# One encoder layer on one core: both heads' products with v as one item of the order, first loads and splits ordered anew, six pairs of the first feed-forward layer begun with plain products

## The chip, the cores and the metric

The kernel runs on one NeuronCore of one Trainium2 chip. The metric is the device time of one execution in microseconds (us). Times come from several runs; one further execution is recorded by the hardware profiler, instruction by instruction, and the rows below come from that one.

## What is computed

One layer of a bidirectional encoder over 1024 positions of width 1024, in float32:

```
z = rms_norm(x) @ W_in + b_in          # split into q | k | v | u | y_branch | g_att | g_rec
y_att = neighbourhood_attention(q, k, v, rpb) @ w_att_o      # 8 heads of 64
y_rec = ((rg_lru forward + rg_lru backward)(conv(u)) * gelu(y_branch)) @ w_rec_o
x = x + (sigmoid(g_att) * y_att + sigmoid(g_rec) * y_rec) @ w_out
x = x + square(relu(rms_norm(x) @ w_ff1)) @ w_ff2
out = rms_norm(x)
```

The attention works on 64 tiles of 128 queries by 384 keys: four pairs of heads (m), two halves of the grid (hf), four column blocks (n), and the two heads of the pair (hd). The probabilities of a tile are multiplied with the v of 384 gathered keys of 64 columns each.

## The kernel before, in words

**Products.** TensorE multiplies pairs of float32r numbers: each operand is split into a high part (a rounded copy, made by ScalarE, sometimes by VectorE) and a low part (the rest, made by VectorE), and a product is three matmuls, high by high, high by low, low by high. The product with W_in (without v's columns) and both feed-forward products are done in seven block products instead of eight. `pairs` does this for a pair of weight blocks: the plain products A11·B11 and A12·B21 need only the first half of the positions, while the five others, S2·T2, S1·T1, S3·T3, S4·B22 and A22·T4, use sums and differences of blocks, which need all positions. The first `pre` pairs do their two plain products ahead of everything else, two pairs at a time; every later pair does its seven in a row. A pair keeps its first bank of PSUM (key 0) from A11·B11 to A22·T4. Before, the `pairs` call of the first feed-forward layer has `pre` 4, that of W_in has 2. A plain product is 12 matmuls of 128x512.

**The order.** Nothing is issued in program order. Every operation is recorded in a `Plan` with a position: a list of products (`main`, one unit of position for each) and side work at fractional positions (`SD(pos, fn, boost)`, a boost moves it ahead). `Plan.solve` is a list scheduler: with its own costs for each operation it lets each engine take, at each moment, the operation with the lowest position among those whose inputs are ready, and hands out the buffers ("t" has 45 tiles of 512 KB in SBUF, "w" 9, PSUM has "pm" 2, "pr" 2, "pa" 4 banks). A bank or a "w" tile is handed out in the order of positions. `Plan.issue` then writes each engine's instructions in the order found. On the chip each engine, and SP's queue, which issues all DMAs, runs that fixed order and waits where an input is late. A transfer's end is estimated from `dma[0]`, when the queue is free, a rate and a latency.

**The start.** x comes in eight tiles (`load_x`), v's weights in four (`wvj`). A tile is squared and summed (`norm1_a`, ScalarE), scaled (`norm1_b`, VectorE, by a chain of small operations, `rstd_chain`), transposed on TensorE against an identity, and split (`put_0` for tiles 0 to 3, `put_F` and `put_D` for 4 to 7). v is the first product. The weights' high parts are made by VectorE for the parts in `WD`, by ScalarE otherwise.

**The attention.** A tile passes `a_qk` (two matmuls, then VectorE and ScalarE make the probabilities), `a_norm`, `a_tr` (three transposes, then ScalarE copies them out of PSUM) and `a_av`. `a_av` runs once for a pair of tiles, head 0 and head 1: three steps b, in each a matmul for head 0 into the lower 64 partitions of a bank and one for head 1 into the upper 64. In the trace each of these plain float32 matmuls leaves two records, so that a pair has 12. Each matmul waits for its own head's transposed tile alone. The attention's positions lie among the 64 steps of the product with w_rec_o (`tprod`, six matmuls a step), which fills TensorE in between.

**The channel part.** x @ w_out is done in tiles of 128 positions; each finished tile is normalised (`ln2`), transposed in "pa" banks, and goes into the blocks B11, B21 (tiles 0 to 3) or the sums T1 to T4 and B22 (tiles 4 to 7) of the first feed-forward product.

Of the kernel before, what the change touches and what calls it, by code (L numbers as in the profile page):

```python
# [10 lines left out]
P = 128  # L11
# [95 lines left out]
class Plan:  # L107


    def __init__(self, slots):  # L110
        self.ops, self.slots, self.pos, self.boost = [], slots, 0.0, 0.0
        self.last_alloc, self.last_tab = {}, None
        self.talloc, self.reserve, self.mark = [], 4, None
        self.late, self.rlate, self.gated = 1e9, 2, False

    def engine(self, name):
        return _Eng(self, name)
# [1 line left out]
    def add(self, eng, meth, args, kw):  # L119
# [21 lines left out]
        for v in wr:  # L141
            t = v.base
            if not t.ops:
                op.alloc.append(t)
                t.first = op.idx
                if t.tag == "t":
                    self.talloc.append(op.idx)
                elif t.tag not in "scd":
                    if t.tag in self.last_alloc:
                        op.preds.setdefault(self.last_alloc[t.tag], 0)  # L150
                    self.last_alloc[t.tag] = op.idx
            for o, b in t.writes:
                if _hit(b, v.box):
                    op.preds[o.idx] = 1
            for o, b in t.reads:
                if o is not op and _hit(b, v.box):
                    op.preds[o.idx] = 1
            t.writes = [(o, b) for o, b in t.writes if not all(x[0] >= y[0] and x[1] <= y[1]
                                                              for x, y in zip(b, v.box))]
            t.writes.append((op, v.box))  # L160
            t.ops.add(op.idx)
        op.preds.pop(op.idx, None)
        if eng == "pe":
            self.mark = op.idx
# [43 lines left out]
    def solve(self):  # L208
# [13 lines left out]
        av = {e: [] for e in engs}  # L222
        parked = {}
        cur = [None]
        dma = [0.0]

        tnext = [0]
        wait = []
# [42 lines left out]
        while done < len(ops):  # L271
# [23 lines left out]
            tfree[e] = s + c  # L295
            op.end = s + c
            if op.bytes:
                dma[0] = max(dma[0], s + 900) + op.bytes / 330.0
                op.end = dma[0] + 1200
            done += 1  # L300
            for t in op.tiles:
                k = id(t)
# [45 lines left out]
def emit(tc, x, prm, wst, wv, wg, watt, wrec, wout, wff1, wff2, tb, bv, lnf, out):  # L348
# [6 lines left out]
    with ExitStack() as ctx:  # L355
# [18 lines left out]
        def PM():  # L374
            return VT(nm("pm"), (P, 512), F32, "pm")
# [63 lines left out]
        dve.memset(epst, EPS)  # L439
        act.activation(s1("tab"), epst, AF.Sqrt)  # L440
        SD(-98, lambda: sp.dma_start(pr, prm))

        def softplus():
            lam = pr[:, PC["lam"]:PC["lam"] + 16]
# [143 lines left out]
        def prod(o, a, ob, b, key, bank, first, ev, boost=5.0):  # L588

            for kk in range(2):  # L590
                def run(kk=kk):
                    if kk == 0 and first:
                        o.ps[key] = PM() if bank else PA()
                    hi, lo = o.lhs[a]()
                    ps = o.ps[key]
                    for k in (2 * kk, 2 * kk + 1):
                        bh, bl = ob[b]["h"][kk][:, k % 2, :], ob[b]["l"][kk][:, k % 2, :]
                        pe.matmul(ps, hi[:, k, :], bh, start=(first and k == 0), stop=False, skip_group_check=True)
                        pe.matmul(ps, hi[:, k, :], bl, start=False, stop=False, skip_group_check=True)
                        pe.matmul(ps, lo[:, k, :], bh, start=False, stop=(k == 3), skip_group_check=True)  # L600
                last = M(run)
            SD(last + 0.1, lambda: ev(o, o.ps[key]), boost)
# [28 lines left out]
            o.store(o.r1, 1)  # L631
            o.store(o.r0, 0)

        def pairs(srcs, stores, ob, pre):

            ps_ = []
            for st in stores:
                o = Obj()
                o.r0, o.store, o.ps = None, st, {}
                ps_.append(o)  # L640
            st = here()
            for i in range(pre):
                pjob(ps_[i], srcs[i], st + 4 * i, st + 4 * pre + 10 * i)
            for i0 in range(0, pre, 2):
                g = ps_[i0:min(i0 + 2, pre)]
                for o in g:
                    prod(o, "A11", ob, "B11", 0, i0 == 0, True, ev1, 30.0)
                for o in g:
                    prod(o, "A12", ob, "B21", 1, False, True, ev2, 30.0)
            for i, o in enumerate(ps_):  # L650
                if i >= pre:
                    pjob(o, srcs[i], here(), here() + 2)
                    prod(o, "A11", ob, "B11", 0, True, True, ev1, 10.0)
                    prod(o, "A12", ob, "B21", 1, False, True, ev2)
                prod(o, "S2", ob, "T2", 0, False, False, ev6)
                prod(o, "S1", ob, "T1", 2, False, True, ev5)
                prod(o, "S3", ob, "T3", 0, False, False, ev7)
                prod(o, "S4", ob, "B22", 2, False, False, ev3)
                prod(o, "A22", ob, "T4", 0, False, False, ev4)
                o.end = here()  # L660
            return [o.end for o in ps_]

# [1 line left out]
            return len(main)  # L664

        hT = Half("hT")
        PRE1, ND, NB = 2, 1, 0.0
        WD, P0B, P0N = (0, 1, 2), 4.0, 2

        xt = [None] * 8  # L670

# [14 lines left out]
        def norm1_b(t):  # L686
            o = nrm[t]
            r = rstd_chain(o.ss, o.s)
            dve.tensor_scalar(o.h, xt[t], r, None, ALU.mult)

        wvj = []
        for i in range(4):
            o = Obj()
# [13 lines left out]
                dve.tensor_sub(o.lo, o.st, o.hi)  # L707

            SD(-90 + i, dma)
            SD((-9, -6, -2.4, -2.3)[i], sp_)  # L710
        SD(-99, lambda: load_x(0))
        SD(-86.5, lambda: sp.dma_start(bvb, bv.unsqueeze(0).broadcast_to((P, 512))))
        for t in range(1, 8):
# [119 lines left out]
                ("g", 4), ("y", 3), ("g", 5), ("u", 3), ("g", 6), ("g", 7), ("qk", 0), ("qk", 1), ("qk", 2), ("qk", 3))  # L833
        FIRST = {"u": 8, "y": 16, "g": 24}
        STORE = {"u": st_u, "y": st_y, "g": st_g, "qk": st_qk}
        RSTEP, RRATE, AOFF, ASTEP = 33.0, 1.0, 1.0, 0.75
        B0 = here()
        ends = pairs([(wst[i], wst[4 + i]) if k == "qk" else (wst[FIRST[k] + 2 * i], wst[FIRST[k] + 2 * i + 1])
                      for k, i in PORD], [STORE[k](i) for k, i in PORD], ob1, PRE1)
# [225 lines left out]
        def a_tr(o):  # L1065
            pt = PA()
            for b in range(3):
                pe.transpose(pt[:, b * P:(b + 1) * P], o.p[:, b * P:(b + 1) * P], ident)
            o.pt = o.t
            act.activation(o.pt, pt[:, :384], AF.Copy)  # L1070

        avb = {}

        def a_av(o0, o1):
            if o0.n == 0:
                avb[0] = PA()
            ps = avb[0]
            for b in range(3):
                g = b + o0.hf
                for o in (o0, o1):  # L1080
                    pe.matmul(ps[o.hd * DH:(o.hd + 1) * DH, o.n * P:(o.n + 1) * P],
                              V[o.m][g // 2][:, g % 2, o.n, o.hd * DH:(o.hd + 1) * DH],
                              o.pt[:, b * P:(b + 1) * P], start=(b == 0), stop=(b == 2))
            if o0.n == 3:
                m, hf = o0.m, o0.hf
                if hf == 0:
# [9 lines left out]
        for s in range(nt):  # L1096
            o = tiles[s]
            if o.n % 2 == 0 and o.hd == 0:
                if s < 4:
                    SD(o.pos - 6, lambda o=o: b_load(o.m, o.hf, o.n // 2))  # L1100
                else:
                    SD(tiles[s - 4].pos + 0.1, lambda o=o: b_load(o.m, o.hf, o.n // 2))
            SD(o.pos, lambda o=o: a_qk(o))
            nxt = [tiles[s + d].pos if s + d < nt else tiles[-1].pos + (s + d - nt + 1) * ASTEP for d in range(4)]
            SD(nxt[1] + 0.1, lambda o=o: a_norm(o))
# [16 lines left out]
            split(rT[k].hi, rT[k].lo, rec[k])  # L1122

        for k in range(8):
            SD(RO - 16 + 1.2 * k, lambda k=k: rec_load(k))
            SD(RO - 9 + 1.2 * k, lambda k=k: rec_split(k))

        def att_load(k):
            att[k] = T("att")
# [192 lines left out]
        def hid(i):  # L1322
            return 4 * (i // 2) + i % 2

        pairs([(wff1[hid(i)], wff1[hid(i) + 2]) for i in range(16)], [ff_store(i) for i in range(16)], ob2, 4)

# [286 lines left out]
```

## Time and profile before

| | |
|---|---|
| median of three runs | 1441.06 us (1440.65 to 1441.09) |
| the profiled execution's own time | 1440.83 us |
| its span, first to last instruction | 1439.0 us |
| TensorE busy | 1413.8 us (98% of the span), 6544 matmuls |
| VectorE, ScalarE busy | 1042.2 us (72%), 854.2 us (59%) |
| granted TensorE clock, mean | 0.998 |
| the 16 DMA engines | 229.04 MB, 159 GB/s in the mean |
| the chain that ended last, by engine | TensorE 97%, DMA 1%, VectorE 1%, ScalarE 1% |

TensorE's busy time is the union of matmuls whose ends are modelled, each shown with its whole passage through the array; the distance from one start to the next tells what a matmul costs the engine. Nearly all instructions are recorded by one helper and so carry one line number (L336); they are told apart by the names of the tiles that they write and read.

### The profile page before, as it was taken

The numbers are of one execution on the slowest core, as the hardware profiler recorded it, in microseconds if no ns is written. First come the engines' busy times: TensorE is split into PE (matmuls) and PEld (weight loads), VectorE is DVE, ScalarE is ACT, GpSimd is POOL, SyncE is SP. The second block draws the span as 40 slices with busy tenths as digits, with TensorE's granted clock in tenths as the row PEclk, the third lists the DMA queues.
The fourth block names the chain that finished last, engine by engine and source line by source line (L and its number), as shares of the span: only waits on it lengthen the run. The fifth ranks groups of instructions, "written<-read, shape, count | busy, mean of one in ns | idle before, by whom it ended". The sixth has DMA issues, their size and how long they took to land.

```text
span 1439.0 us, 17698 instructions
## 1 busy us (share of the span) xinstructions
PE 1413.8 (98%) x6544; PEld 1159.2 (81%) x6544; DVE 1042.2 (72%) x1590; ACT 854.2 (59%) x1321; POOL 0.7 (0%) x6
## 2 busy tenths in 40 slices
PE   6999999999999999999999999999999999999997
PEld 5878888888888877777888788888888888888886
DVE  6897688896986777664855776666655877858996
ACT  7758786878668766654526555455555634322544
POOL 0000000000000000000000000000000000000000
PEclk9999999999999999999999999999999999999999
DMA  6523234234224866544903325444447883245402
GB/s 214 146 74 132 103 103 146 83 123 146 102 90 157 310 220 233 176 166 181 399 31 117 117 92 194 161 161 161 161 153 256 303 331 118 90 151 200 140 22 103
DMA packets 86936, 229.04 MB, mean 159 GB/s; under 512 B 8513, under 2 KB 16833, under 8 KB 86849
## 3 DMA queue, kind: packets, MB, share of 16 engines
q1 hardware_dynamic: 86848, 227.91, 45.5%
q8 instruction: 51, 0.84, 0.2%
q14 instruction: 37, 0.30, 0.1%
HBM read 158.67 MB, written 69.21 MB: 158 GB/s over the span
## 4 chain that ended last, share of the span: by engine, by line
PE 97%; DMA 1%; DVE 1%; ACT 1%; issue 0%; SPq 0%
PE pa L336 56%; PE pm L336 33%; PE pr L336 8%; DMA x<-in_x_dram 1%; DMA ws<-in_wv_dram 0%; ACT h L336 0%; DVE T4l L336 0%; DVE T1l L336 0%; ACT hTh L336 0%; DVE h L336 0%; ACT r L336 0%; DVE sl L336 0%; ACT ns L336 0%; DVE nu L336 0%; ACT F L336 0%
## 5 line engine op out<-in xcount | busy, mean ns | idle before, releaser
L336 PE MATMUL pa<-wh,rh 128*128 128x512 f32 x448 | 173.9, 389 | 0.0
L336 PE MATMUL pa<-wh,rl 128*128 128x512 f32 x448 | 173.9, 389 | 0.0
L336 PE MATMUL pa<-wl,rh 128*128 128x512 f32 x448 | 173.8, 389 | 0.0
L336 ACT ACTIVATE r<-r 128x1024 f32<-128x1024 f32 x64 | 67.7, 1060 | 68.2 <-DVE r L336 66.9
L336 ACT ACTIVATE r<-pm 128x512 f32<-128x512 f32 x102 | 60.4, 592 | 73.7 <-PE pm L336 72.8
L336 DVE TENSOR_TENSOR sl<-ws,sh 128x1024 fp32r<-128x1024 f32 x72 | 87.4, 1221 | 22.9 <-ACT sh L336 22.9
L336 ACT ACTIVATE rh<-rs 128x1024 fp32r<-128x1024 f32 x56 | 58.5, 1048 | 67.1 <-PE pa L336 53.5
L336 PEld LDWEIGHTS pa<-wh,rh 128*128 128x128 f32 x448 | 84.1, 188 | 17.5
L336 PEld LDWEIGHTS pa<-wh,rl 128*128 128x128 f32 x448 | 84.1, 188 | 17.5
L336 PEld LDWEIGHTS pa<-wl,rh 128*128 128x128 f32 x448 | 84.1, 188 | 17.3
L336 ACT ACTIVATE wh<-w 128x1024 fp32r<-128x1024 f32 x56 | 58.8, 1051 | 60.2 <-PE pa L336 43.9
L336 ACT ACTIVATE sh<-ws 128x1024 fp32r<-128x1024 f32 x72 | 75.6, 1056 | 31.0 <-DVE ws L336 25.1
L336 DVE TENSOR_TENSOR wl<-ws,wh 128x1024 fp32r<-128x1024 f32 x64 | 77.5, 1218 | 17.1 <-ACT wh L336 16.5
L336 PE MATMUL pm<-T4h,wx 128*128 128x512 f32 x272 | 89.5, 389 | 0.0
L336 DVE TENSOR_TENSOR r<-pa,r 128x512 f32<-128x512 f32 x74 | 50.9, 688 | 50.2 <-PE pa L336 48.3
L336 DVE TENSOR_TENSOR acc<-pa,acc 128x512 f32<-128x512 f32 x72 | 49.4, 688 | 50.4 <-PE pa L336 50.3
L336 DVE TENSOR_TENSOR wl<-w,wh 128x1024 fp32r<-128x1024 f32 x56 | 68.2, 1219 | 10.1 <-ACT wh L336 6.7
L336 ACT ACTIVATE wh<-ws 128x1024 fp32r<-128x1024 f32 x61 | 64.0, 1055 | 13.4 <-DMA ws<-in_wff_dram 6.8
L336 DVE TENSOR_TENSOR rl<-rs,rh 128x1024 fp32r<-128x1024 f32 x56 | 68.2, 1219 | 5.2 <-ACT rh L336 3.0
L336 DVE CUSTOM_DVE_ANT_0 ab<-pa,B 128x384 f32<-128x384 f32 x64 | 35.4, 556 | 39.6 <-PE pa L336 38.8
L336 PEld LDWEIGHTS pm<-T4h,wx 128*128 128x128 f32 x272 | 51.1, 188 | 10.6
L336 ACT ACTIVATE ab<-pa 128x384 f32<-128x384 f32 x64 | 31.0, 484 | 45.6 <-PE pa L336 45.4
(242 smaller groups left out, 3776.1 us busy)
## 6 DMA issues: line engine op xcount, KB each, us to landing
rs<-rd SPq DMA_DIRECT2D x56, 512.0 KB, 6.6
ws<-in_wst_dram SPq DMA_DIRECT2D x41, 512.0 KB, 4.1
ws<-in_wff_dram SPq DMA_DIRECT2D x36, 512.0 KB, 4.5
w<-in_wff_dram SPq DMA_DIRECT2D x32, 512.0 KB, 7.5
B<-in_tb_dram SPq DMA_DIRECT2D x32, 384.0 KB, 4.6
x<-in_x_dram SPq DMA_DIRECT2D x16, 512.0 KB, 9.0
gd<-r SPq DMA_DIRECT2D x16, 512.0 KB, 2.9
g<-gd SPq DMA_DIRECT2D x16, 512.0 KB, 8.2
```

Of the source, the lines that this page charges most:

```text
L336: getattr(eng[op.eng], op.meth)(*[r(a) for a in op.args], **{k: r(a) for k, a in op.kw.items()})
```

## The change

`a_av` makes all six matmuls of a pair of tiles wait for both heads' transposed tiles (`plan.also`). 24 transposes of the identity are added at the very start (`warm`). The estimate of transfers in the scheduler is changed (700 ns, 290 bytes/ns and 1500 ns in place of 0, 330 and 1200), the positions of the first two v splits and the boosts of the first tiles are changed, ScalarE makes the high parts of all of v's weights, and VectorE the second copy of two tiles in place of one. The loads of the attention's bias tiles are six tiles ahead in place of four, the loads and splits of the recurrent branch's result lie earlier, and the attention's positions are moved ahead by 7 units. In the first feed-forward product six pairs begin with plain products in place of four; the first bank of pairs alternates between "pm" and "pr" (pairs 4 and 5 have theirs in "pa").

```diff
@@ -111,7 +111,7 @@
         self.talloc, self.reserve, self.mark = [], 4, None
-        self.late, self.rlate, self.gated = 1e9, 2, False
+        self.late, self.rlate, self.gated, self.also = 1e9, 2, False, ()
@@ -159,6 +159,8 @@
             t.ops.add(op.idx)
+        for o in self.also:
+            op.preds[o.idx] = 1
         op.preds.pop(op.idx, None)
@@ -222,7 +224,7 @@
         cur = [None]
-        dma = [0.0]
+        dma = [700.0]
@@ -295,8 +297,8 @@
             if op.bytes:
-                dma[0] = max(dma[0], s + 900) + op.bytes / 330.0
-                op.end = dma[0] + 1200
+                dma[0] = max(dma[0], s + 900) + op.bytes / 290.0
+                op.end = dma[0] + 1500
             done += 1
@@ -440,6 +442,14 @@
+        def warm():
+            ps = PA()
+            for _ in range(NWARM):
+                pe.transpose(ps[:, :P], ident, ident)
+
+        NWARM = 24
+        SD(-97, warm)
+
         def softplus():
@@ -590,7 +600,7 @@
                     if kk == 0 and first:
-                        o.ps[key] = PM() if bank else PA()
+                        o.ps[key] = VT(nm(bank), (P, 512), F32, bank)
                     hi, lo = o.lhs[a]()
@@ -631,12 +641,13 @@
-        def pairs(srcs, stores, ob, pre):
+        def pairs(srcs, stores, ob, pre, banks=("pm",)):
...
                 o.r0, o.store, o.ps = None, st, {}
+                o.bank = banks[len(ps_) % len(banks)] if len(ps_) < 2 * len(banks) or len(ps_) >= pre else "pa"
                 ps_.append(o)
@@ -644,19 +655,19 @@
                 for o in g:
-                    prod(o, "A11", ob, "B11", 0, i0 == 0, True, ev1, 30.0)
+                    prod(o, "A11", ob, "B11", 0, o.bank, True, ev1, 30.0)
                 for o in g:
-                    prod(o, "A12", ob, "B21", 1, False, True, ev2, 30.0)
+                    prod(o, "A12", ob, "B21", 1, "pa", True, ev2, 30.0)
             for i, o in enumerate(ps_):
...
                     pjob(o, srcs[i], here(), here() + 2)
-                    prod(o, "A11", ob, "B11", 0, True, True, ev1, 10.0)
-                    prod(o, "A12", ob, "B21", 1, False, True, ev2)
-                prod(o, "S2", ob, "T2", 0, False, False, ev6)
-                prod(o, "S1", ob, "T1", 2, False, True, ev5)
-                prod(o, "S3", ob, "T3", 0, False, False, ev7)
-                prod(o, "S4", ob, "B22", 2, False, False, ev3)
-                prod(o, "A22", ob, "T4", 0, False, False, ev4)
+                    prod(o, "A11", ob, "B11", 0, o.bank, True, ev1, 10.0)
+                    prod(o, "A12", ob, "B21", 1, "pa", True, ev2)
+                prod(o, "S2", ob, "T2", 0, None, False, ev6)
+                prod(o, "S1", ob, "T1", 2, "pa", True, ev5)
+                prod(o, "S3", ob, "T3", 0, None, False, ev7)
+                prod(o, "S4", ob, "B22", 2, None, False, ev3)
+                prod(o, "A22", ob, "T4", 0, None, False, ev4)
                 o.end = here()
@@ -664,8 +675,8 @@
         hT = Half("hT")
-        PRE1, ND, NB = 2, 1, 0.0
-        WD, P0B, P0N = (0, 1, 2), 4.0, 2
+        PRE1, PRE2, ND, NB = 2, 6, 2, 2.0
+        WD, P0B, P0N = (), 8.0, 4
@@ -688,6 +699,7 @@
+        W0P, W1P = -5.4, -5.2
         wvj = []
@@ -707,7 +719,7 @@
             SD(-90 + i, dma)
-            SD((-9, -6, -2.4, -2.3)[i], sp_)
+            SD((W0P, W1P, -2.4, -2.3)[i], sp_)
         SD(-99, lambda: load_x(0))
@@ -833,7 +845,7 @@
         STORE = {"u": st_u, "y": st_y, "g": st_g, "qk": st_qk}
-        RSTEP, RRATE, AOFF, ASTEP = 33.0, 1.0, 1.0, 0.75
+        RSTEP, RRATE, AOFF, ASTEP = 33.0, 1.0, -6.0, 0.75
         B0 = here()
@@ -1067,7 +1079,7 @@
             o.pt = o.t
-            act.activation(o.pt, pt[:, :384], AF.Copy)
+            o.done = act.activation(o.pt, pt[:, :384], AF.Copy)
@@ -1075,12 +1087,14 @@
             ps = avb[0]
+            plan.also = (o0.done, o1.done)
             for b in range(3):
...
                               o.pt[:, b * P:(b + 1) * P], start=(b == 0), stop=(b == 2))
+            plan.also = ()
             if o0.n == 3:
@@ -1096,10 +1110,10 @@
             if o.n % 2 == 0 and o.hd == 0:
-                if s < 4:
+                if s < 6:
                     SD(o.pos - 6, lambda o=o: b_load(o.m, o.hf, o.n // 2))
                 else:
-                    SD(tiles[s - 4].pos + 0.1, lambda o=o: b_load(o.m, o.hf, o.n // 2))
+                    SD(tiles[s - 6].pos + 0.1, lambda o=o: b_load(o.m, o.hf, o.n // 2))
             SD(o.pos, lambda o=o: a_qk(o))
@@ -1122,8 +1136,8 @@
         for k in range(8):
-            SD(RO - 16 + 1.2 * k, lambda k=k: rec_load(k))
-            SD(RO - 9 + 1.2 * k, lambda k=k: rec_split(k))
+            SD(RO - 24 + 2 * k, lambda k=k: rec_load(k))
+            SD(RO - 12 + 2 * k, lambda k=k: rec_split(k))
@@ -1322,7 +1336,7 @@
-        pairs([(wff1[hid(i)], wff1[hid(i) + 2]) for i in range(16)], [ff_store(i) for i in range(16)], ob2, 4)
+        pairs([(wff1[hid(i)], wff1[hid(i) + 2]) for i in range(16)], [ff_store(i) for i in range(16)], ob2, PRE2, ("pm", "pr"))
...

```

## Rows read from the trace of the kernel before

**Rows 1.** Windows of 36 us: length, busy us (instructions) of each engine, clock, DMA.
```profile
0.00:36.00 36.00, 24.42 (x109) 19.52 (x110) 23.71 (x75) 26.27 (x79) 0.70 (x6) 1.00 0.63 214
...
72.00:108.00 36.00, 34.32 (x149) 27.48 (x148) 32.93 (x78) 19.87 (x26) 0.00 (x0) 1.00 0.24 73
108.00:144.00 36.00, 36.00 (x160) 29.80 (x160) 27.19 (x27) 30.50 (x36) 0.00 (x0) 1.00 0.39 132
...
576.00:612.00 36.00, 36.00 (x224) 27.15 (x222) 22.34 (x70) 24.30 (x56) 0.00 (x0) 1.00 0.57 176
...
792.00:828.00 36.00, 32.63 (x151) 27.14 (x150) 25.71 (x61) 21.57 (x61) 0.00 (x0) 0.96 0.32 117
```

**Rows 2.** Waits of TensorE: who for whom, us in total, times, longest.
```profile
PE pa L336 <- DVE h L336: 15.3, 3, 10.7
```

**Rows 3.** Timeline of TensorE in the attention: start us, length, instructions merged.
```profile
516.79 0.34 PE L336 MATMUL pa<-kl,qs 128*128 128x384 f32 x1
516.97 0.39 PE L336 MATMUL pm<-rl,wh 128*128 128x512 f32 x1
...
517.94 0.34 PE L336 MATMUL pa<-kl,qs 128*128 128x384 f32 x1
518.21 0.87 PE L336 MATMUL pa<-ab,V 128*64 128x128 f32 x6
519.01 0.50 PE L336 MATMUL pm<-rh,wl 128*128 128x512 f32 x1
519.35 0.39 PE L336 MATMUL pr<-rh,wl 128*128 128x512 f32 x1
...
539.70 0.88 PE L336 MATMUL pa<-ab,V 128*64 128x128 f32 x12
...
551.71 0.43 PE L336 MATMUL pa<-ab,V 128*64 128x128 f32 x2
552.07 0.55 PE L336 MATMUL pa<-ident,ab 128*128 128x128 f32 x3
552.55 0.87 PE L336 MATMUL pa<-ab,V 128*64 128x128 f32 x10
```

**Rows 4.** Timeline of all engines at the start; in brackets the idle time before.
```profile
5.93 0.16 DVE L336 RECIPROCAL nr<-ns 128x1 f32<-128x1 f32 x1 [0.17 <-ACT ns L336]
...
7.45 0.69 DVE L336 CAST wh<-ws 128x1024 fp32r<-128x1024 f32 x1 [1.36 <-DMA ws<-in_wv_dram]
9.76 0.75 DVE L336 TENSOR_SCALAR h<-x,nr 128x1024 f32<-128x1024 f32 x1
...
10.65 1.94 PE L336 MATMUL pa<-ident,h 128*128 128x128 f32 x8 [10.65 <-DVE h L336]
...
12.25 1.20 PE L336 MATMUL pm<-wh,hTh 128*128 128x512 f32 x2
...
16.08 0.69 PE L336 MATMUL pm<-wl,hTh 128*128 128x512 f32 x2
```

**Rows 5.** Timeline of TensorE, 55 to 57 us.
```profile
55.55 1.09 PE L336 MATMUL pa<-ident,h 128*128 128x128 f32 x8 [1.26 <-DVE h L336]
56.40 0.47 PE L336 MATMUL pa<-hTh,wh 128*128 128x512 f32 x1
```

**Rows 6.** Timeline of TensorE around the start of the feed-forward layer.
```profile
825.13 1.96 PE L336 MATMUL pa<-ident,h 128*128 128x128 f32 x8 [3.37 <-DVE h L336]
826.75 0.78 PE L336 MATMUL pa<-B21h,wh 128*128 128x512 f32 x1
...
828.60 0.39 PE L336 MATMUL pa<-B21l,wh 128*128 128x512 f32 x1
```

**Rows 7.** Costliest groups (busy us, mean ns, idle before) and DMA issues (count, KB, us to landing), from the page.
```profile
L336 DVE TENSOR_TENSOR sl<-ws,sh 128x1024 fp32r<-128x1024 f32 x72 | 87.4, 1221 | 22.9 <-ACT sh L336 22.9
...
L336 ACT ACTIVATE sh<-ws 128x1024 fp32r<-128x1024 f32 x72 | 75.6, 1056 | 31.0 <-DVE ws L336 25.1
...
rd<-r SPq DMA_DIRECT2D x16, 512.0 KB, 3.1
```

## The prediction

> **What bounds the kernel now.** I read the windows first. From 108 us on TensorE is busy in every microsecond of every window but two, that of 792 to 828 us and the last; in the first it lacks 11.6 us, in the third 1.7 [rows 1], in the second 1.26 [rows 5]. So time can be won in two ways only: where TensorE idles, or where it is busy with something that need not take so long. The waits of TensorE name the idle time: 15.3 us in three waits for a normalised tile h [rows 2]. The timeline shows them: 10.65 us at the start [rows 4], 1.26 us at 54 us [rows 5], 3.37 us at 822 us [rows 6].
>
> For the busy part I went through the attention on TensorE's timeline, start to start. A 512-column matmul takes 0.23 us (160 in a full window of 36 us [rows 1]). Six records of the product with v, one head's three matmuls, take 0.80 us (518.21 to 519.01); twelve records, both heads', are no longer: the merged rows are 0.87 and 0.88 us long [rows 3]. The heads write different halves of the partitions, and when they stand next to each other they run at once. When something stands between them each head pays the full 0.80 us, and no idle time shows it.
>
> **The pairs of heads.** I counted all stretches of these records between the first (515.69 us) and the last (666.50 us): 384 records in 58 stretches, 29 of 6, 11 of 12, 8 of 2, 6 of 4, 3 of 10, 1 of 8. From the start of each stretch to the start of what follows, they take 41.5 us together. Besides, the first of a stretch comes 0.27 us after a short matmul that a plain one follows in 0.18 (517.94 to 518.21, 516.79 to 516.97), and what follows it is slow, 0.34 in place of 0.23 us (519.01 to 519.35) [rows 3]: 0.09 + 0.11 = 0.20 us a stretch. The whole now is 41.5 + 58 x 0.20 = 53.1 us.
>
> After the change all six matmuls of a pair become ready together, so that they stand together unless an operation of lower position becomes ready meanwhile. One can: the transposes of the next tile stand 0.1 ahead in the order. Rows show it: 2 records, three transposes, then the other 10 take 0.36 us (551.71 to 552.07) and once more a whole group's 0.80 (a row of 0.87 us) [rows 3]. That the 10 stand in one piece shows that both heads were ready when the 2 began, so that the new rule would not have mended this pair. Among the pairs that were ready together in the trace, 16, I count 5 cut in this way and 11 whole. Taken over to 32 pairs: 22 whole at 0.81, 10 cut at about 1.25 us (between 0.36 + 0.80 and 0.58 + 0.81), 42 stretches: 17.8 + 12.5 + 42 x 0.20 = 38.7 us. **That is -14.4 us.** The bounds: no pair cut, 32 x 1.01 = 32.3, -20.8 us; twice as many cut, 12 x 0.81 + 20 x 1.25 + 52 x 0.20 = 45.1, -8.0 us. I take the middle since nothing in the diff touches the next tile's transposes.
>
> [...]
>
> The pair now waits for the later head. Behind it TensorE's queue would stand still, but the order puts steps of the w_rec_o product there, 384 matmuls x 0.23 = 87 us of filler, and in these windows VectorE and ScalarE work 22.3 and 24.3 of 36 us [rows 1]; 15 us less leaves both under 80%. I cost this wait at nothing; without the filler it would be a transpose's copy, some 0.5 us a pair. The attention's move by 7 units, the earlier loads, the deeper bias prefetch, and the scheduler's new estimate of transfers reorder work on all queues, SP's too, and cost nothing where TensorE has no idle time to fill (108 to 792 us). If they make one late load, each costs a wait like the 1.26 us one; bounds -2 to +6 us.
>
> **The start.** The first tile's chain is ready to go on at 6.1 us (reciprocal at 5.93 us), but VectorE's next instruction is the copy of the first v weights, which waits for its transfer until 7.45 us; then the chain takes until 9.76 us, when h begins, because the weights' low part lies between [rows 4]. With the two splits at later positions and the copies on ScalarE, chain and scaling follow at once: 0.7 us, an estimate for four small operations at the 0.16 us of the reciprocal's row, h from 6.8 us, transposes at 6.8 + 0.89 (from 9.76 to 10.65) = 7.7 us: -3.0 us. [...] The 24 new transposes run from about 1.5 us, where nothing else can, for 24 x 0.20 = 4.8 us, and end 1.4 us before h comes; after an idle time of 1.26 us the clock was still up (0.85 us for eight) [rows 5], after 3.37 us it was down (1.62) [rows 6]. I take it as up. That makes -5.2 us, but v's later weights come one after another on the same queue, are split by busier engines and may hold the first tile's products. **I take -4**, bounds 0 (these weights set the pace either way) and -7 (the second tile's products fill the holes too).
>
> [...]
>
> **The feed-forward layer.** The wait of 3.37 us is for the last tile's h. Next in order are products into "pa", which are handed out in order, behind the banks for that tile's transposes. After it the clock is down until 828.6 us [rows 6]: eight transposes 1.62 in place of 0.85, four matmuls from 826.75 to 828.60 in place of 0.91 us: 0.8 + 0.9 = 1.7. Together 5.1 us. With "pr" as a second set of banks, A11·B11 of pairs 2 and 3 can run ahead of the tile: 24 matmuls x 0.23 = 5.5 us, more than 3.37. They need two more splits by then, 2 x 1.06 on ScalarE and 2 x 1.22 on VectorE [rows 7], and there the window has 14 and 10 us free of 36 [rows 1]. **I take -5**, bounds -1 (splits late) and -5.1. The two pairs more cost one more transfer of 512 KB each at 32% DMA share.
>
> **Sum.** -14.4 - 4 - 5 = -23.4 us on 1440.83, the profiled execution's own time (span 1439.0 and 1.8 around it; the median is 0.2 us above it): 1417.4 us.
>
> **Rivals.** *The cuts multiply:* the new order brings the next tile's transposes into nearly every pair, for they become ready while the pair's group runs. The 5 of 16 cut pairs speak for it, the 11 whole ones against. 32 cut pairs cost 32 x (1.25 + 0.40) = 52.8 us, as now: 1440.8 - 0.3 - 9 = 1431.5 us.
> *The start gives nothing:* weights or clock hold it; 1421.4 us.
> *Six held pairs run out of SBUF, slower:* six first results and the 28 tiles of the seven blocks take 34 of 45 "t" tiles; a pair's split sums take 4, its outputs 3. If the next pair's splits must wait until a pair's outputs are stored, each boundary shows a store of 3.1, then 1.06 and 1.22 us, 5.4 us [rows 7]; five boundaries are 27 us: 1417.4 + 27 = 1444.4 us. It decides only if fewer than four tiles are free when the next splits are due; by the count 45 - 34 - 4 - 3 = 4 remain, so it is just avoided.
> *Everything fits:* no cuts, the start -7: 1440.8 - 20.8 - 7 - 5.1 = 1407.9 us.
> *New waits from the reordering* in stretches now full, half the gain: 1429 us.
>
> **How the numbers follow.** Chances: the forecast 0.58, the start nothing 0.10, cuts 0.10, everything fits 0.08, new waits 0.07, SBUF 0.07. The bound of 0.2% (about 2.9 us, what a measurement of this kernel can tell from no change) lies at 1438.2 and 1443.9: only the SBUF case reaches it, and part of the new waits. Faster 0.91, same 0.03, slower 0.06. The forecast's own spread (-8 to -20.8, 0 to -7, -1 to -5.1, not all at one end) is 1409 to 1427; to leave out no more than 2 in 10 the range goes up to the cuts and new waits at the middle of their prices: 1408 to 1430. Predicted: 1417.5 us.
>
> **What would show it.** Right: records of the product with v in about 42 stretches, most of 12; the first transposes of h at about 7.7 us at the upper clock; no wait for h at 822 us, matmuls of pairs 2 and 3 in "pm" and "pr" before the last tile's transposes; TensorE's count of matmuls up by 24. Wrong: stretches of 6 or 2 and 10 everywhere; TensorE idle in windows that were full, above all behind a late transfer or between the first pairs of the feed-forward layer; waits for v's low parts in the first 20 us that eat the earlier start.

## The result, and the profile after

The changed kernel takes 1419.4 us (median; 1418.8 to 1420.5), the kernel before in the same rounds 1441.0 us: a ratio of 0.9851, 95% interval 0.9834 to 0.9868. The profiled execution took 1419.77 us with a span of 1418.0, 21.0 us less than the span before. Every ratio in this document is taken against the kernel before in the same rounds; its median lay between 1439.8 and 1441.0 us from one set of rounds to the next, so that a difference of about 1 us between two runs is not shown by their times alone.

Windows of the changed kernel, as in [rows 1]: length, busy us and instructions of each engine, granted clock, DMA share, GB/s.

```profile
0.00:36.00 36.00, 30.81 (x138) 24.91 (x139) 23.16 (x73) 27.00 (x75) 0.70 (x6) 0.91 0.63 216
72.00:108.00 36.00, 33.32 (x145) 26.62 (x144) 32.89 (x77) 20.08 (x26) 0.00 (x0) 1.00 0.19 59
...
576.00:612.00 36.00, 36.00 (x241) 28.89 (x239) 28.12 (x72) 25.40 (x54) 0.00 (x0) 1.00 0.66 226
792.00:828.00 36.00, 36.00 (x168) 29.70 (x167) 30.21 (x64) 22.79 (x58) 0.00 (x0) 1.00 0.42 145
```

Three things answer to [rows 1]. TensorE is now full from 792 to 828 us. In the attention (576 to 612 us) it was full and is full, but holds 241 instructions in place of 224: the same busy time does more. From 72 to 108 us it is busy 33.32 us, 1.00 less than before, while VectorE is as busy as it was.

The waits of TensorE, as in [rows 2]:

```profile
PE pa L338 <- DVE h L338: 2.2, 1, 2.2
PE pa L338 <- POOL ident L338: 1.4, 1, 1.4
PE pa L338 <- DVE T1l L338: 1.3, 1, 1.3
PE pm L338 <- ACT wh L338: 1.0, 1, 1.0
PE pm L338 <- ACT r L338: 0.7, 1, 0.7
PE pa L338 <- ACT r L338: 0.7, 1, 0.7
PE pm L338 <- DVE wl L338: 0.6, 1, 0.6
```

Of the 15.3 us for a tile h, 2.2 are left. New are the waits for T1l (0.3 us before), wh and the identity.

TensorE's timeline in the attention, to be laid beside [rows 3]: one pair of heads whole, and one cut.

```profile
634.67 0.88 PE L338 MATMUL pa<-ab,V 128*64 128x128 f32 x12
635.48 0.44 PE L338 MATMUL pa<-kh,qs 128*128 128x384 f32 x1
...
637.42 0.43 PE L338 MATMUL pa<-ab,V 128*64 128x128 f32 x2
637.79 0.55 PE L338 MATMUL pa<-ident,ab 128*128 128x128 f32 x3
638.26 0.87 PE L338 MATMUL pa<-ab,V 128*64 128x128 f32 x10
639.06 0.45 PE L338 MATMUL pa<-kh,qs 128*128 128x384 f32 x1
```

The first pair runs both heads in 0.81 us (634.67 to 635.48). The second has begun when the next tile's transposes become ready and go in between: 0.37 and 0.80 us. I counted the stretches again: 384 records in 42, 22 of them of 12; 10 pairs are cut. From start to start they take 29.4 us (41.5 before).

The start, TensorE's timeline, beside [rows 4]:

```profile
1.35 4.25 PE L338 MATMUL pa<-ident 128*128 128x128 f32 x24 [1.35 <-POOL ident L338]
7.79 1.97 PE L338 MATMUL pa<-ident,h 128*128 128x128 f32 x8 [2.18 <-DVE h L338]
9.40 1.20 PE L338 MATMUL pm<-wh,hTh 128*128 128x512 f32 x2
...
13.14 0.73 PE L338 MATMUL pm<-wh,hTh 128*128 128x512 f32 x2 [1.04 <-ACT wh L338]
14.46 1.18 PE L338 MATMUL pm<-wl,hTh 128*128 128x512 f32 x2 [0.59 <-DVE wl L338]
```

h's transposes come at 7.79 us, 2.86 us earlier, but at the lower clock level (1.97 us at a granted clock of 0.50; at 1.00 it is 1.09 [rows 5]). The windows of the same execution show that level from 7.7 to 11.1 us and again from 14.5 to 18.0:

```profile
7.70:11.10 3.40, 3.31 (x12) 2.77 (x12) 2.23 (x6) 2.16 (x9) 0.00 (x0) 0.50 1.03 414
11.10:14.50 3.40, 1.76 (x6) 0.64 (x5) 3.40 (x10) 3.40 (x8) 0.00 (x0) 1.00 0.90 351
14.50:18.00 3.50, 3.50 (x9) 2.74 (x10) 3.40 (x11) 3.21 (x6) 0.00 (x0) 0.51 1.02 412
```

And the start of the feed-forward layer, beside [rows 6]:

```profile
802.28 0.39 PE L338 MATMUL pm<-B11h,wh 128*128 128x512 f32 x1
...
802.96 0.39 PE L338 MATMUL pr<-B11h,wh 128*128 128x512 f32 x1
...
809.01 1.09 PE L338 MATMUL pa<-ident,h 128*128 128x128 f32 x8
809.86 0.48 PE L338 MATMUL pa<-B21h,wh 128*128 128x512 f32 x1
```

Products into "pm" and "pr" fill the time until the last tile's h; its transposes wait for nothing and run at the upper level (granted clock 1.00 from 809.01 to 809.86 us).

**Where the time went.** I set the starts of the same matmul in both traces beside each other. The last T4 product of the second pair of the first projection starts at 107.00 us (108.28 before): the start gives 1.3 us. From there to the last product with w_rec_o, which closes the attention, it is 556.00 us (570.73): 14.7. From the last product with w_out to the last T4 product of the feed-forward layer it is 303.74 us (308.73): 5.0. What lies between and behind them is unchanged; the three make the 21.0 us of the span.

### The profile page after: what moved, and what is told of

Its sections match the earlier page's. It is cut to its first block, busy times and chain, and to the rows that moved or that the text cites. A ratio compares the mean times of both kernels' runs of the same rounds, so it can differ in the third digit from the quotient of the medians.

```text
span 1418.0 us, 17748 instructions
## 1 busy us (share of the span) xinstructions
PE 1402.9 (99%) x6568; PEld 1153.0 (81%) x6568; DVE 1041.9 (73%) x1595; ACT 852.0 (60%) x1316; POOL 0.7 (0%) x6
## 4 chain that ended last, share of the span: by engine, by line
PE 98%; DVE 1%; ACT 0%; DMA 0%; issue 0%
PE pa L338 57%; PE pm L338 28%; PE pr L338 13%; DMA x<-in_x_dram 0%; DVE T4l L338 0%; DVE T1l L338 0%; ACT F L338 0%; DVE F L338 0%; ACT hTh L338 0%; ACT h L338 0%; DVE wl L338 0%; DVE sl L338 0%; DVE hTl L338 0%; DVE T3l L338 0%; DVE nu L338 0%
## 5 line engine op out<-in xcount | busy, mean ns | idle before, releaser
L338 ACT ACTIVATE r<-pm 128x512 f32<-128x512 f32 x81 | 48.0, 592 | 52.5 <-PE pm L338 51.8
L338 ACT ACTIVATE wh<-ws 128x1024 fp32r<-128x1024 f32 x64 | 67.2, 1055 | 15.6 <-DMA ws<-in_watt_dram 8.4
L338 PE MATMUL pm<-T4h,wx 128*128 128x512 f32 x216 | 71.4, 389 | 0.0
L338 PE MATMUL pa<-T1l,sh 128*128 128x512 f32 x144 | 56.2, 390 | 1.3 <-DVE T1l L338 1.3
L338 PE MATMUL pa<-T1h,sh 128*128 128x512 f32 x144 | 56.1, 389 | 0.0
L338 PE MATMUL pa<-T1h,sl 128*128 128x512 f32 x144 | 56.0, 389 | 0.0
```

The costliest lines, as they stand in the source:

```text
L338: getattr(eng[op.eng], op.meth)(*[r(a) for a in op.args], **{k: r(a) for k, a in op.kw.items()})
```

## Experiments on the attention

My theory was that the gain is both heads running at once; the rival, that the move and the earlier loads bring it. The first run is the kernel before with nothing but the join, the second the changed kernel without it.

```
 (kernel before)
+            o.done = act.activation(o.pt, pt[:, :384], AF.Copy)
+            plan.also = (o0.done, o1.done)     # around the six matmuls
```

> The kernel before, with only the join: both heads' products with v wait for both heads' last copies. The theory (the gain is the heads running at once): about 42 stretches of these records in place of 58, 29 us from start to start in place of 41.5, and the whole 14.4 us: about 1426.5 us. The rival (the joined item gains only together with the attention's move by 7 units and the earlier loads): stretches near 58, or waits in place of them, 1438 to 1441 us.

```
 (changed kernel)
-            plan.also = (o0.done, o1.done)
```

> The changed kernel without the join alone. The theory: the stretches go back to about 58 and the time rises by some 14.4 us, to about 1434 us. The rival (the move and the new load order do it): it stays within 3 us of 1419.4.

The join alone gave 1421.4 us, 0.9874 (0.9861 to 0.9888); without it the changed kernel took 1435.2 us, 0.9970 (0.9959 to 0.9982). So the join is the attention's gain, and by itself it gained 18 us, not 14.4: more than in the changed kernel, where it has company. What takes some back? The attention stands 7 units earlier in the changed kernel's order:

```
 (changed kernel)
-        RSTEP, RRATE, AOFF, ASTEP = 33.0, 1.0, -6.0, 0.75
+        RSTEP, RRATE, AOFF, ASTEP = 33.0, 1.0, 1.0, 0.75
```

> The changed kernel with the attention at its former place in the order (7 units later). The join alone left 37 stretches, the changed kernel has 42. First theory (the move is what makes the five more cuts): some 37 stretches and 29.4 + 42 x 0.20 - 27.2 - 37 x 0.20 = 3.2 us less: 1416.2 us. Rival (the earlier loads or the scheduler's new estimate of transfers make them): 42 stretches, 1419.4 us.

It gave 1417.2 us, 0.9840 (0.9827 to 0.9854), 2.2 us less than the changed kernel. The last one puts the products with v ahead of the next tile's transposes, which stood at nxt[3] + 0.2:

```
 (changed kernel)
-                SD(nxt[3] + 0.3, lambda o0=tiles[s - 1], o1=o: a_av(o0, o1))
+                SD(nxt[3] + 0.15, lambda o0=tiles[s - 1], o1=o: a_av(o0, o1))
```

> The changed kernel with the products with v placed ahead of the next tile's transposes in the order. First theory (those transposes are what cuts ten pairs): no pair cut, 32 stretches, from 29.4 + 42 x 0.20 = 37.8 to 32 x 1.01 = 32.3 us, so about 5.5 us less, 1413.9 us. Rival (the transposes become ready first and cut as before, or are now late and make waits of their own): 42 stretches or new waits, 1418 to 1421 us.

It gave 1413.7 us, 0.9812 (0.9798 to 0.9825). All 32 pairs are whole; a pair's end on TensorE's timeline of this run:

```profile
632.88 0.88 PE L338 MATMUL pa<-ab,V 128*64 128x128 f32 x12
633.69 0.55 PE L338 MATMUL pa<-ident,ab 128*128 128x128 f32 x3
```

The transposes that cut ten pairs now follow the twelve records.

The forecast's sum can be put to all of them: time inside the stretches, from start to start, plus 0.20 us for each. The last column is the stretch of time defined above (second pair's last T4 product to the last product with w_rec_o), against the 570.73 us of before.

| kernel | stretches (of 12) | inside, us | sum against before | measured |
|---|---|---|---|---|
| before | 58 (11) | 41.5 | | |
| without the join | 56 (10) | 42.4 | +0.5 | +1.3 |
| changed | 42 (22) | 29.4 | -15.3 | -14.7 |
| attention moved back | 38 (26) | 27.7 | -17.8 | -16.8 |
| join only | 37 (27) | 27.2 | -18.5 | -18.3 |
| products with v first | 32 (32) | 25.8 | -20.9 | -20.5 |

Every row agrees within about 1 us. The 0.20 us a stretch, read off neighbours in [rows 3], carries 26 x 0.20 = 5 of the 20.5 us of the last row, and without it the last three rows would miss by 3 to 5 us. Taken from the measured column instead, each of the last four rows by itself gives 0.15 to 0.19 us a stretch. What this price consists of, no run here shows.

## Experiments on the feed-forward layer

```
 (changed kernel)
-        pairs(..., ob2, PRE2, ("pm", "pr"))     # PRE2 = 6
+        pairs(..., ob2, 4, ("pm",))
```

> The changed kernel with four pairs of the feed-forward layer ahead and one set of banks, as before. The theory: the wait for the last tile's h and the lower clock behind it come back, +5.0 us, 1424.4 us. The rival (the attention's shorter time has moved the tiles so that the wait is gone anyway): no change, 1419.4 us.

```
+        pairs(..., ob2, 4, ("pm", "pr"))
```

> The changed kernel with four pairs ahead but two sets of banks. If the second set of banks is what lets products run ahead of the last tile, the products of pairs 2 and 3 still stand ahead of it and the time is that of the changed kernel, 1419.4 us. If six pairs are needed, the wait comes back in part or whole: 1421 to 1424.4 us.

Four pairs and one set of banks: 1424.3 us, 0.9891 (0.9878 to 0.9905), 4.9 us more than the changed kernel. The old wait is back, and the lower clock level behind it (1.97 us for the eight transposes; mean granted clock from 792 to 828 us 0.95, before 0.96 [rows 1]):

```profile
808.73 1.97 PE L338 MATMUL pa<-ident,h 128*128 128x128 f32 x8 [3.37 <-DVE h L338]
```

Four pairs and two sets of banks: 1422.9 us, 0.9883 (0.9870 to 0.9897). The products do run ahead and the wait for h shrinks to 0.65 us, but TensorE is through with the plain products sooner and reaches the first pair's product with T2 at 824.07 us (827.30 with one set of banks), before VectorE has made that product's low parts:

```profile
808.65 1.09 PE L338 MATMUL pa<-ident,h 128*128 128x128 f32 x8 [0.65 <-DVE h L338]
...
824.07 0.50 PE L338 MATMUL pm<-T2h,sh 128*128 128x512 f32 x1 [0.24 <-ACT sh L338]
826.71 0.50 PE L338 MATMUL pm<-T2h,sl 128*128 128x512 f32 x1 [1.90 <-DVE sl L338]
```

0.65 + 0.24 + 1.90 = 2.79 us in place of 3.37. By the marks above the layer takes 308.39 us with one set of banks and 307.09 with two, against 303.74. In the changed kernel the two more pairs put this product off to 834.02 us, and it waits for nothing. So with four pairs the second set of banks mostly moves the wait. Six pairs with one set of banks were not run: that both edits are needed is argued from the order of the products, not shown.

## Experiments on the start

Without the transposes of the identity:

```
 (changed kernel)
-        SD(-97, warm)
```

> The changed kernel without the 24 transposes at its start. First theory (the clock has fallen again when h comes, so they are worth nothing): the first transposes of h at 7.8 us as now, 2.0 us long, and 1419.4 us within 0.5. Rival (they lift the clock for some of the first products after all): 1.5 to 2.2 us more, 1421 to 1421.6 us.

It took 1420.9 us (1419.4 to 1421.8), 0.9861 (0.9848 to 0.9875): 1.4 us more, with ranges that touch. In the profiles the second pair ends 1.2 us later than in the changed kernel's own (table below). That lies on the rival's side, though I had expected nothing. But the run does not tell what the transposes are worth: without them the scheduler finds another order. ScalarE squares the second tile, at 8.58 us, ahead of its copies of h's transposes, which begin at 9.64 us in place of 8.94, and the first product begins at 10.04 us in place of 9.40.

With more of them:

```
 (changed kernel)
-        NWARM = 24
+        NWARM = 46
```

> 46 transposes in place of 24, so that TensorE works until h comes. First theory (the idle time after them is what brought the clock down): the first transposes of h at the upper clock, 1.0 us in place of 2.0, the first products at 0.23 us, and the end earlier by 0 to 1.6 us, little of it since VectorE's splits set the pace between 72 and 88 us: 1418 to 1419.4 us. Rival (46 of them delay h's own transposes, or the clock stays low): 1419.4 us or up to 1 us more.

It took 1423.8 us, 0.9882 (0.9868 to 0.9895): 4.4 us more, and neither theory had that. The 22 further transposes were to fill an idle time of 2.18 us, 0.10 us each; all 46 took 8.12 us, 0.18 us each:

```profile
1.36 8.12 PE L338 MATMUL pa<-ident 128*128 128x128 f32 x46 [1.36 <-POOL ident L338]
9.32 1.04 PE L338 MATMUL pa<-ident,h 128*128 128x128 f32 x8
13.13 0.73 PE L338 MATMUL pm<-wh,hTh 128*128 128x512 f32 x2 [2.77 <-ACT wh L338]
```

h's transposes ran at the upper level (1.04 us, granted clock 1.00 from 7.7 to 11.1 us), as the first theory had it, but 1.5 us later, and the first product with v waited 2.77 us for ScalarE's copy of its weights. Again the order is another. In the changed kernel ScalarE makes that copy while TensorE waits for h:

```profile
6.62 1.06 ACT L338 ACTIVATE wh<-ws 128x1024 fp32r<-128x1024 f32 x1 [0.57 <-DMA ws<-in_wv_dram]
```

With 46 transposes it stands behind the copies of h's transposes, and ScalarE idles for 3.99 us before them:

```profile
9.96 2.18 ACT L338 ACTIVATE hTh<-pa,pr 128x128 fp32r<-128x128 f32 x8 [3.99 <-PE pa L338]
11.97 1.10 ACT L338 ACTIVATE wh<-ws 128x1024 fp32r<-128x1024 f32 x1
```

So the run tells nothing of a clock held up to 7.7 us; that wasn't tried with fewer of them.

With four pairs of the first projection begun with plain products, to cover the waits behind 79 us:

```
 (changed kernel)
-        PRE1, PRE2, ND, NB = 2, 6, 2, 2.0
+        PRE1, PRE2, ND, NB = 4, 6, 2, 2.0
```

> The changed kernel with four pairs of the first projection begun with plain products in place of two. First theory (the waits of 0.69, 1.30 and 0.69 us between 79 and 88 us are for splits, and plain products can stand there): up to 2.7 us less, 1416.7 to 1418.5 us. Rival (the two more pairs' weight splits are on the same VectorE and ScalarE and make other waits): 1419.4 us or up to 3 us more.

It took 1421.2 us (1420.0 to 1425.8), 0.9871 (0.9854 to 0.9887): no gain. The three waits are gone and others stand in their place, 2.04 us for sl at 88.58 us and 2.22 for sh at 245.31. Two of the lines of this run's waits:

```profile
PE pa L338 <- DVE sl L338: 2.2, 2, 2.0
PE pm L338 <- ACT sh L338: 2.2, 1, 2.2
```

The kernel before with only the start's edits:

```
 (kernel before)
+        SD(-97, warm)                                # 24 transposes
-        PRE1, ND, NB = 2, 1, 0.0
+        PRE1, ND, NB = 2, 2, 2.0
-        WD, P0B, P0N = (0, 1, 2), 4.0, 2
+        WD, P0B, P0N = (), 8.0, 4
-            SD((-9, -6, -2.4, -2.3)[i], sp_)
+            SD((-5.4, -5.2, -2.4, -2.3)[i], sp_)
```

> The kernel before with the edits of the start alone: 24 transposes of the identity first, the first v weights' splits at their later place, the copies on ScalarE. First theory (the marks of the profiles: h 2.5 us earlier, 1.1 us of it given back at the waits between 78 and 90 us): about 1.4 us less than before. The forecast's term: 4 us less. Rival: nothing at all, within 0.5 us.

It took 1440.6 us (1437.1 to 1441.2) against 1440.6 us (1437.8 to 1442.1): 0.9997 (0.9988 to 1.0006). For this start that excludes the 4 us of the forecast; the 1.4 us lie just inside the interval, whose edge is 1.7 us, and nothing at all lies in its middle. Two things limit what it says. The profiled execution was the shortest of the eleven, 1437.1 us, so its marks are not those of the median. And the run lacks the scheduler's new estimate of transfers: its order departs from the changed kernel's at TensorE's 77th instruction after the transposes of the identity, so it is not quite that kernel's start.

Why is an h that comes 2.9 us earlier worth so little? VectorE's timeline of the changed kernel, before the wait for T1l at 84.12 us:

```profile
77.82 1.21 DVE L338 TENSOR_TENSOR sl<-ws,sh 128x1024 fp32r<-128x1024 f32 x1
78.95 2.76 DVE L338 TENSOR_TENSOR T4l<-F,T4h 128x256 fp32r<-128x256 f32 x8
81.64 2.76 DVE L338 TENSOR_TENSOR T1l<-F,T1h 128x256 fp32r<-128x256 f32 x8
84.32 0.68 DVE L338 TENSOR_TENSOR wx<-ws,wx 128x512 fp32r<-128x512 f32 x1
```

VectorE works without a gap, and makes T4's low parts first although the product with T1 comes before that with T4. The next run swaps them, on top of the run with the products with v first; the last one puts the old start into that kernel.

```
 (products with v first)
-        SD(32.5, lambda: put_1((("T4", 0, 4), ("T1", 0, 0))))
+        SD(32.5, lambda: put_1((("T1", 0, 0), ("T4", 0, 4))))
```

> The run with the products with v ahead of the next tile's transposes (1413.7 us) with one more edit: of the first layer's right-hand operands, T1's parts are made before T4's. First theory (VectorE's eight subtractions for T4l and eight for T1l, 5.4 us in a row, hold TensorE at the T1 product): the wait of 1.3 us for T1l at 83 us is gone, T1l being made 2.7 us earlier, and no other takes its place, 1412.4 us. Rival (VectorE's work as a whole sets the pace there, and the wait only moves on to T4l or the next splits): 1413.7 us.

```
 (the run above)
-        SD(-97, warm)
-        PRE1, PRE2, ND, NB = 2, 6, 2, 2.0
+        PRE1, PRE2, ND, NB = 2, 6, 1, 0.0
-        WD, P0B, P0N = (), 8.0, 4
+        WD, P0B, P0N = (0, 1, 2), 4.0, 2
-        W0P, W1P = -5.4, -5.2
+        W0P, W1P = -9, -6
```

> The fastest run so far (products with v ahead of the next tile's transposes, T1's parts before T4's; 1412.0 us) with the start of the kernel before: no transposes of the identity, the first v weights' splits and the copies where they were. It measures the start's worth in a kernel without the wait for the last tile's h, whose times scatter by less than 1 us. First theory (by the marks the start is worth 1.4 us behind 90 us): 1413.4 us. Second theory (VectorE's T4l ahead of T1l was what gave 1.1 us back, and is mended here): 2.4 us, 1414.4 us. Rival (the start gives nothing, as the run with the start alone showed within 1.3 us): 1412.0 us. The forecast's term: 1416.0 us.

The swap gave 1412.0 us (1411.6 to 1412.3), 0.9803 (0.9790 to 0.9817), the fastest kernel here; the wait for T1l is gone and no other of its size took its place. In the profiles the second pair ends 0.7 us earlier (105.90 and 105.21). With the old start it took 1412.6 us (1412.4 to 1413.4), 0.9808 (0.9795 to 0.9821). So in this kernel the start is worth 0.6 us by the medians, nearest to the rival; the two intervals overlap widely, so that it can't be told from nothing. This run keeps the new estimate of transfers, and its order is not that of the kernel before either. Starts of matmuls on TensorE's timelines, us:

| kernel | h's transposes | first T2 product | second pair's last T4 product |
|---|---|---|---|
| before | 10.65 | 78.29 | 108.28 |
| join only (old start) | 9.40 | 77.18 | 107.16 |
| start only | 7.64 | 74.61 | 106.29 |
| changed | 7.79 | 76.00 | 107.00 |
| five others with the changed kernel's start | 7.36 to 7.59 | 74.91 to 75.36 | 105.90 to 106.35 |
| no transposes of the identity | 7.69 | 76.53 | 108.17 |
| 46 of them | 9.32 | 80.25 | 111.35 |
| v first, T1 first | 7.43 | 75.23 | 105.21 |
| the same, old start | 9.29 | 76.31 | 105.14 |

The five are the runs without the join, with the attention moved back, with the products with v first, and with four pairs and one or two sets of banks: up to 105 us TensorE, VectorE and ScalarE have the changed kernel's instructions in its order.

The last two rows end at the same place. The new start is 1.08 us ahead at the first T2 product and has lost it when the second pair ends. TensorE's waits in between are 1.67 us with the new start and 1.12 with the old:

```profile
79.03 0.50 PE L338 MATMUL pm<-T3h,sh 128*128 128x512 f32 x1 [0.69 <-ACT r L338]
85.22 0.50 PE L338 MATMUL pa<-hTh,sh 128*128 128x512 f32 x1 [0.69 <-ACT r L338]
89.43 0.50 PE L338 MATMUL pa<-hTh,wh 128*128 128x512 f32 x1 [0.29 <-ACT wh L338]
```

```profile
78.16 0.50 PE L338 MATMUL pm<-T2h,sl 128*128 128x512 f32 x1 [1.12 <-DVE sl L338]
```

All these waits are for splits and copies on VectorE and ScalarE. Their idle time accounts for 0.55 of the 1.15 us. They cost more than their idle time, for the starts around them are slow as well (with the new start 0.34 us from each of the three to the next): from start to start, against 0.227 us a matmul, the stretch between the two marks loses 2.54 us with the new start and 1.63 with the old. That is 0.91; the other 0.23 is one T1 product that the old start's order has ahead of the first mark.

## Why the prediction was right, point by point

The forecast was 23.4 us less; the profiles show 21.0, the medians 21.6. The mechanism of all three parts held; the start is the term that was too large.

**The pairs of heads: right in size, not wholly in its reasons.** -14.4 us were predicted, -14.7 measured, with the predicted 42 stretches, 22 of them whole. But the forecast carried 5 cut pairs of 16 over to 10 of 32 and gave as its reason that nothing in the diff touches the next tile's transposes. The count itself is uncertain: counted again, the trace of before has three pairs of 2 and 10 records and one of 4 and 8 beside the 11 whole ones, 4 of 15. The join alone leaves 5 cut pairs of 32 and gives -18.3 us. The move of the attention brings most of the other cuts (moved back, 6 pairs are cut) and costs 2 us. The step that I costed at nothing, since it only reorders work where TensorE has no idle time, had a price without a wait. Two errors of opposite sign cancelled: that the 42 stretches came out to the number is luck.

**The start: the term that was mis-sized.** -4 predicted, -1.3 in the two profiles, 0 to 0.6 by the times of the two runs made for it, whose orders differ from these kernels'. The -1.3 is the distance of two single executions. With the five others of the changed kernel's start (105.90 to 106.35) against the two executions of the old one (107.16 and 108.28) it is 0.8 to 2.4 us. All stay well under 4. Its first step held (transposes at 7.7 us predicted, 7.79 measured), but the profile of before has them late: in two other executions with the old start they came at 9.29 and 9.40 us, not 10.65. "I take it as up" failed in the changed kernel's profile, after 2.18 us of idle time (granted clock 0.50). In the other runs with the 24 transposes the idle time was 0.85 to 1.35 us and h's transposes ran at the upper level (1.09 or 1.10 us); six of the eight then had a stretch of the lower one a few us later (a granted clock of 0.50 in one or more windows of 1.7 us), behind waits for copies and splits. The other two, without the join and with the attention moved back, stayed at the upper level (1.00 in every window from 5.9 to 18 us), and it brought nothing: the products that would have been slow wait instead. With the attention moved back the fourth pair of records of the first product begins at 12.97 us, in the changed kernel at 13.14, and the second pair ends at 106.02 us, among the others' 105.90 to 106.35.

```profile
12.97 0.73 PE L338 MATMUL pm<-wh,hTh 128*128 128x512 f32 x2 [0.95 <-ACT wh L338]
```

The five starts bring h 1.8 to 3.3 us earlier than the two old ones, the last matmul of v 1.8 to 3.4 (64.71 to 65.16 us against 66.98 and 68.09) and the second pair's end 0.8 to 2.4. Of the sum's -5.2 us, 3.0 are the earlier h; the other 2.2 it put on the clock level of the first transposes and products, a term that no run shows. The profile of before has these slow, 1.60 us for the eight, at a recorded clock of 1.00; and with the new starts v's end comes earlier by about as much as h and no more, and about 1 us more went at the waits for splits and copies from 78 us on. Where the sum said "v's later weights may hold the first products" it named a right place; more is held later, at 78 to 90 us, by the splits for the first pairs.

**The feed-forward layer: right.** -5 predicted, -5.0 measured, with no wait, the products in "pm" and "pr" and the upper level. Of these 3.4 us are the wait and 1.6 the lower level behind it in the profile of before; against an execution in which the clock stayed up (307.10 us, below) the edit gives 3.4. The rival that SBUF runs out showed nowhere: TensorE is full from 792 to 828 us.

**The rivals.** "The start gives nothing" (1421.4) was as near as the forecast: the median, 1419.4 us, lies 2.0 below the one and 1.9 above the other. "The cuts multiply" came true in small, through the move. "Everything fits" shows what was left: without cuts another 5.7 us. "New waits from the reordering" did not come: from 108 to 792 us the changed kernel's TensorE has none. That the filler would leave VectorE room was read off one window, with 22.3 us; the other three of the attention have 24.7 to 26.5, and it sufficed there too.

## What to carry to other kernels

A busy engine is not a full one (here 241 matmuls in place of 224 in the same 36.00 busy us): count how often its records change their kind, and price each change from neighbours in the timeline; here such a sum agreed with five kernels within about 1 us, with no idle time to point at. Ask of each moved step not only what will wait for it but also what it will stand between. An earlier start is worth only what the engines that feed the next stage can follow (here 1.08 us at the first T2 product, nothing at the second pair's end), and one profile of it can be a microsecond off (107.16 and 108.28 us with the old start): look at the same mark in several executions before a term is made of it. Where a scheduler finds the order, a run that takes one edit out can change the order of everything: compare the engines' sequences before its time is put down to the edit.

## What the runs showed of the hardware

**One idle time, both clock levels.** The same wait of 3.37 us for the last tile's h left TensorE's eight transposes at 1.96 us in the kernel before [rows 6] (granted clock 0.52 from 825.1 to 826.7 us) and at 1.97 with four pairs and one set of banks, but at 1.09 with the start alone and at 1.12 with the join alone:

```profile
823.09 1.09 PE L336 MATMUL pa<-ident,h 128*128 128x128 f32 x8 [3.37 <-DVE h L336]
```

```profile
805.78 1.12 PE L338 MATMUL pa<-ident,h 128*128 128x128 f32 x8 [3.37 <-DVE h L338]
806.63 0.71 PE L338 MATMUL pa<-B21h,wh 128*128 128x512 f32 x1
```

In the second of these the lower level came with the next matmuls (granted clock 0.53 from 806.6 to 810.2 us). In the first it came not at all (1.00 from 823 to 831 us), and from the last w_out product to the layer's last T4 product it took 307.10 us in place of 308.73. So this wait costs its own length, and 0 to 1.6 us more by the clock. The same idle time, then, settles neither whether the lower level comes nor when; what does, no run here shows.

**The first transposes.** The 24 ran at 0.18 to 0.22 us each (4.25 to 5.38 us in all), as slowly as the changed kernel's eight of h at a granted clock of 0.50 (1.61 us from the first start to that of the next matmul, 0.20 each), while the changed kernel's record shows a granted clock of 1.00 for them (1.35 to 5.60 us). In the kernel before it shows 1.00 as well from 10.65 to 16.10 us, where eight transposes take 1.60 us and a matmul 0.5 [rows 4]. In these two stretches of the start the recorded level is not what the durations say.
